# Nine instead of seven of 22 up-projection chunks by seven products, taken in pairs, with weights prepared in two stages

## The chip, the cores and the metric

The kernel runs on one core of a Trainium2 chip. The metric is the device time of one execution in microseconds (us). The core has five engines that each work through a list of their own in order: PE multiplies matrices, DVE does elementwise arithmetic on two operands, ACT does copies and activation functions, POOL and SP here mostly issue DMAs. An engine waits on semaphores for the others. PE writes its results into PSUM, which has eight banks of 128 x 512 f32; everything else is in SBUF.

## The reference, cut to what matters

The program is a decoder trunk of two layers on a residual stream of 512 x 1024. Each layer ends in a gated feed-forward block whose first half is what the change touches:

```python
def conv_ffn(xn, w_up, cw, cb, w_down):
    a = xn @ w_up                      # 512 x 1024 by 1024 x 5632
    T = a.shape[1]
    ap = jnp.pad(a, ((0, 0), (CONV_W - 1, 0), (0, 0)))
    a = sum(ap[:, j:j + T] * cw[j] for j in range(CONV_W)) + cb
    gate, val = jnp.split(a, 2, axis=-1)
    return (jax.nn.gelu(gate, approximate=True) * val) @ w_down
```

All inputs are f32, and the product must keep nearly f32 accuracy.

## The kernel before, in words

**Products.** An f32 operand is split into a high part, rounded to fp32r, and a low part, which is the rest. A product is then three matmuls (`mm3`, L262): high by high, high by low, low by high. Only the third one reads the low part of the weight.

**Chunks.** In `ffn` (L584) the 5632 columns of the up-projection are taken as 22 chunks (`NF`). Chunk c has 128 gate columns and the 128 value columns that belong to them, and a PSUM bank of 128 x 512 for each. A **plain** chunk takes 2 halves x 8 blocks of 128 rows x 3 matmuls = 48 matmuls of 512 columns. Chunks 0 and 1 are made by `first_products`; the loop at L883 makes chunks 2 to 21.

**Seven products.** For the chunks in `SEVEN` (L27: 6, 8, ..., 18) a chunk is a 2 x 2 block product in Strassen's form (Winograd's variant): seven products A11, A12, S1, S2, S3, S4 and A22 of half the rows and half the tokens, each 4 x 3 matmuls of 256 columns (`half_mm`, L863), 84 in all. Their weights are sums and differences of the four blocks of the chunk's weights. `seven_weights` (L650) makes them: raw weights r0 and r1, sums sa and sb (four DVE additions of 512 columns), then four tiles w[0] to w[3] of high parts (ACT copies) and low parts (DVE subtractions). The four output quarters o1 to o4 lie in two banks, and five small DVE additions (L908, L909, L916, L921, L923) with one ACT copy (L906, s1) join the seven products; a product that accumulates onto a quarter can start only when the addition that reads the quarter has run.

**Order within a chunk.** Each engine's order is the program's order (a schedule written by hand). During chunk c the engines also treat the results of chunk c-1: `taps` (L589: per bank one ACT activation, L593, and two DVE multiply-adds, L594 and L596), `glu` (L613, the gelu on ACT) and, a chunk later, `product` (L604, the gate times the value on DVE; the one before goes to DRAM with a POOL DMA, hD, L609). And they prepare the weights of chunk c+2: `weights(c + 2)` is a generator, and each `next(steps)` puts one more step of it into the lists. Near the end of a seven-product chunk PE does the first four blocks of the next plain chunk's first half (`begun`, L917) before S4.

**Weights of plain chunks.** `Weights` (L32) loads raw weights by SP DMAs (L46), 512 KB each, a few ahead; `high` copies the high part on ACT (L54), `low` subtracts on DVE (L62). `high_added` (L81) does without DVE: after the high part ACT writes the negated raw weight, rounded to fp32r, into the place of the low part (L56), and a POOL DMA adds the raw weight to it there (L77, `accum_op=ALU.add`), which leaves the low part. Before the change only chunks 20 and 21 take their weights so, and four weights in the second layer's attention.

**Buffers.** Weight tiles are 8 KB a partition, from a pool of 16 (`t8`); eight of these hold the inputs and their sums during the loop. Raw weights, sa, sb and the taps' bb come from a pool of 10 (`t4`), one of which a gain row holds. A load or a DVE addition that needs a buffer waits until the last reader of an older one is done.

Of the kernel before, what the change touches and what calls it, by code (L numbers as in the profile page):

```python
# [1 line left out]

# [13 lines left out]
T = 512  # L16
# [7 lines left out]
BIG = 3.0e38  # L24


SEVEN = range(6, 19, 2)  # L27
ND = NF // 2
LAST = 3

# [66 lines left out]
def trunk_kernel(ctx, tc, x, norm_gains, w_qkv_a, w_o_a, w_q_b, w_o_b, kv_norm, w_kvf, b_f,  # L97
# [11 lines left out]
    def t8(shape, dt=F32, name="t8"):  # L109
        return p8.tile(shape, dt, tag="t8", name=name)  # L110
# [4 lines left out]
    def t2(shape, dt=F32, name="t2"):  # L115
        return p2.tile(shape, dt, tag="t2", name=name)

    def bank(shape, name="bank"):
        return psp.tile(shape, F32, tag="ps", name=name)
# [464 lines left out]
    def ffn(l, bd, cp, nxt, ahead):  # L584
# [4 lines left out]
        def taps(c, banks, between=None):  # L589
            bb = t4([128, 2, T], name="bb")  # L590
            for s, ch in ((0, c), (1, NF + c)):
                ps = banks[s]
                act.activation(bb[:, s, :], ps, AF.Identity, bias=cp[:, 3, ch:ch + 1], scale=cp[:, 2, ch:ch + 1])  # L593
                dve.scalar_tensor_tensor(bb[:, s, 1:], ps[:, :T - 1], cp[:, 1, ch:ch + 1], bb[:, s, 1:],  # L594
                                         ALU.mult, ALU.add)
                dve.scalar_tensor_tensor(bb[:, s, 2:], ps[:, :T - 2], cp[:, 0, ch:ch + 1], bb[:, s, 2:],  # L596
                                         ALU.mult, ALU.add)
                if s == 0 and between is not None:
                    between()
            return bb  # L600
# [3 lines left out]
        def product():  # L604

            if gated:
                c, bb = gated.pop()
                if c - 1 in hc:
                    pool.dma_start(hD[c - 1], hc.pop(c - 1))  # L609
                hc[c] = t2([128, T], name="hc")  # L610
                dve.tensor_tensor(hc[c], bb[:, 0, :], bb[:, 1, :], ALU.mult)  # L611
# [5 lines left out]
        def post(c, banks, between=None):  # L617
            product()
            glu(c, taps(c, banks, between))
# [4 lines left out]
        def sums_in():  # L624

            v = [t8([128, 4, T], name=f"xsum{i}") for i in range(2)]
            for i in range(2):
                pool.tensor_tensor(v[i], xT[0][i].bitcast(F32), xT[1][i].bitcast(F32), ALU.add)
            yield
            dve.tensor_tensor(v[0][:, :, LO], v[0][:, :, HI], v[0][:, :, LO], ALU.subtract)  # L630
            dve.tensor_tensor(v[0][:, :, HI], v[1][:, :, HI], v[0][:, :, HI], ALU.subtract)
            yield
            dve.tensor_tensor(v[1][:, :, HI], v[1][:, :, HI], v[0][:, :, LO], ALU.subtract)
            dve.tensor_tensor(v[1][:, :, LO], v[1][:, :, LO], v[1][:, :, HI], ALU.subtract)
            yield
            for X, src in ((XA, v[0]), (XB, v[1])):
                X += [t8([128, 4, T], F32R, name="xsh"), t8([128, 4, T], F32R, name="xsl")]
                for k in (0, 2):
                    act.copy(X[0][:, k:k + 2], src[:, k:k + 2])
                    dve.tensor_tensor(X[1][:, k:k + 2], src[:, k:k + 2], X[0][:, k:k + 2].bitcast(F32), ALU.subtract)  # L640
                    yield

        halves = {}

        def split_pair(pair, src, n=1024):
            act.copy(pair[:, 0, :n], src)
            yield
            dve.tensor_tensor(pair[:, 1, :n], src, pair[:, 0, :n].bitcast(F32), ALU.subtract)

        def seven_weights(c):  # L650

            r0, r1 = W.take(2)
            w = [t8([128, 2, 1024], F32R, name="w") for _ in range(4)]
            sa, sb = (t4([128, 1024], name="wsum") for _ in range(2))
            a11, a12, a21, a22 = r0[:, 0:512], r0[:, 512:1024], r1[:, 0:512], r1[:, 512:1024]
            act.copy(w[0][:, 0], r0)
            dve.tensor_tensor(sa[:, 0:512], a11, a21, ALU.subtract)
            dve.tensor_tensor(sb[:, 0:512], a21, a22, ALU.add)
            yield
            dve.tensor_tensor(sa[:, 512:1024], sb[:, 0:512], a11, ALU.subtract)  # L660
            act.copy(w[1][:, 0], sa)
            dve.tensor_tensor(sb[:, 512:1024], a12, sa[:, 512:1024], ALU.subtract)
            yield
            dve.tensor_tensor(w[1][:, 1], sa, w[1][:, 0].bitcast(F32), ALU.subtract)
            act.copy(w[2][:, 0], sb)
            yield
            dve.tensor_tensor(w[0][:, 1], r0, w[0][:, 0].bitcast(F32), ALU.subtract)
            act.copy(w[3][:, 0, 0:512], a22)
            yield
            dve.tensor_tensor(w[2][:, 1], sb, w[2][:, 0].bitcast(F32), ALU.subtract)  # L670
            yield
            dve.tensor_tensor(w[3][:, 1, 0:512], a22, w[3][:, 0, 0:512].bitcast(F32), ALU.subtract)
            v = [t.rearrange("p s (q k c) -> p s q k c", q=2, k=4) for t in w]
            halves[c] = dict(A11=v[0][:, :, 0], A12=v[0][:, :, 1], S3=v[1][:, :, 0], S2=v[1][:, :, 1],
                             S1=v[2][:, :, 0], S4=v[2][:, :, 1], A22=v[3][:, :, 0])

        def plain_weights(c):
            for _ in range(2):
                if c < NF - 2:
                    W.high()  # L680
                    W.low()
                else:
                    W.high_added()
                yield

        def weights(c):
            return seven_weights(c) if c in SEVEN else plain_weights(c)

# [187 lines left out]
        W.ahead = 1  # L878
        W.split(base + 8)
        extra = sums_in()  # L880
        begun = None
        before = None
        for c in range(2, NF):  # L883
            if c == NF - 4:
                pair_load(0)
            if c == NF - 3:
                sums = down_sums([(l, ND - 1), (1, 8 + l)], in_one, pool, 1, 0)
                next(sums)
            steps = weights(c + 2) if c + 2 < NF else iter(())
            banks = [bank([128, T], name="up") for _ in range(2)]  # L890
            if c in SEVEN:
                w = halves.pop(c)
                W.n_get += 2
                x11, x21, x22 = [(xT[0][i], xT[1][i], s) for i, s in ((0, LO), (1, LO), (1, HI))]
                o1, o2, o3, o4 = banks[0][:, LO], banks[0][:, HI], banks[1][:, LO], banks[1][:, HI]
                s1, s12, s17 = (t2([128, 256], name="csum") for _ in range(3))

                def prod(o, a, x, start=False):
                    half_mm(o, w[a], x[0:2], x[2], start)

                prod(o1, "A11", x11, True)
                prod(o2, "S2", (*XB, HI))
                prod(o3, "S3", (*XA, HI), True)
                product()
                bb = taps(*before)
                act.copy(s1, o1)  # L906
                next(steps)
                dve.tensor_tensor(s12, o2, s1, ALU.add)  # L908
                dve.tensor_tensor(s17, o3, s1, ALU.add)  # L909
                glu(before[0], bb)  # L910
                prod(o1, "A12", x21)
                prod(o2, "S1", (*XA, LO))
                prod(o3, "A22", (*XB, LO))
                next(steps)
                next(steps, None)
                dve.tensor_tensor(o4, o2, s17, ALU.add)  # L916
                begun = W.get(), bank([128, T], name="up")  # L917
                up(*begun, range(4))
                prod(o2, "S4", x22)
                next(steps, None)  # L920
                dve.tensor_tensor(o3, o3, s12, ALU.add)  # L921
                next(steps, None)
                dve.tensor_tensor(o2, o2, s1, ALU.add)  # L923
            else:
                for s in range(2):
                    if s == 0 and begun:
                        w, banks[0] = begun
                        up(*begun, range(4, KD))
                        begun = None
                    else:  # L930
                        up(W.get(), banks[s], range(KD))
                    if c == NF - 2:
                        next(sums)
                    if s == 0 and before:
                        post(*before, (lambda: pair_lows(0)) if c == NF - 1 else None)
                        if c >= NF - 2:
                            pair_highs(c - NF + 2)
                            pair_sums(c - NF + 3)
                    next(steps, None)
                    next(extra, None)  # L940
            run(steps)
            before = c, banks
            if c == NF - 3:
                pair_sums(0)
# [725 lines left out]
```

## Time and profile before

| what | value |
|---|---|
| median of three runs | 1122.29 us (1121.77 to 1123.04) |
| the profiled execution's own time | 1126.29 us |
| its span in the profile | 1124.5 us |
| granted PE clock | 0.997 of full speed |
| PE busy | 1110.3 us |
| DVE busy | 892.2 us |
| ACT busy | 614.6 us |
| POOL busy | 183.2 us |

The span runs from the first to the last instruction. Matmuls overlap one another, so the time that one takes from start to end is longer than the distance between two starts; the distance is what counts. In an instruction row the numbers are start and duration in us; in a group row, after the count, busy us and the mean ns of one, then the idle time of the engine ahead of it. In the first layer the loop over chunks 2 to 21 runs from 205.53 to 417.86 us of the span.

### The profile page before, as it was taken

How to read it: one execution, taken by the hardware profiler on the slowest of the kernel's cores; microseconds unless marked ns; L12 is line 12 of the kernel's file. 1: busy time of each engine (PE TensorE's matmuls, PEld its weight loads, DVE VectorE, ACT ScalarE, POOL GpSimd, SP SyncE). 2: the span in 40 equal slices, each digit the busy share in tenths (PEclk: the TensorE clock that was granted, in tenths of full speed). 3: DMA queues.
4: the chain of work that ended last, by engine and by line, in shares of the span. 5: the costliest groups of instructions: out<-in, count | busy, mean ns of one | idle time of the engine just before them, and what ended most of it. 6: DMA issues, size and time to landing. Idle time of an engine off the chain costs nothing.

```text
span 1124.5 us, 17257 instructions
## 1 busy us (share of the span) xinstructions
PE 1110.3 (99%) x6259; PEld 951.7 (85%) x6259; DVE 892.2 (79%) x1453; ACT 614.6 (55%) x1036; POOL 183.2 (16%) x277
## 2 busy tenths in 40 slices
PE   9999999999999999999999999999999999999997
PEld 6988889889899888888788878789989989887886
DVE  6667788888888689997696877748888888689994
ACT  5444575544444556576562678746445445456572
POOL 1832101200000121000001645500300000121000
PEclk9999999999999999999999999999999999999999
DMA  9469854343443699793438666374333433599862
GB/s 322 150 216 409 315 170 134 94 123 113 138 124 114 168 346 377 278 337 104 141 126 305 180 168 156 95 207 122 105 98 118 131 123 121 149 351 371 313 244 75
DMA packets 179183, 217.34 MB, mean 193 GB/s; under 512 B 11225, under 2 KB 131017, under 8 KB 179098
## 3 DMA queue, kind: packets, MB, share of 16 engines
q1 hardware_dynamic: 169594, 183.99, 50.4%
q0 software_dynamic: 9504, 32.25, 8.8%
q8 instruction: 49, 0.80, 0.3%
q14 instruction: 36, 0.29, 0.1%
HBM read 166.08 MB, written 39.63 MB: 183 GB/s over the span
## 4 chain that ended last, share of the span: by engine, by line
PE 83%; DMA 5%; issue 4%; DVE 4%; POOL 2%; ACT 1%; DVEq 0%; POOLq 0%; SPq 0%; ACTq 0%
PE up L263 12%; PE up L264 12%; PE up L265 12%; PE acc L263 8%; PE acc L265 8%; PE acc L264 8%; DMA dact<-hD 3%; PE qk_ps L264 2%; PE qk_ps L263 2%; PE qk_ps L265 2%; PE v_ps L263 2%; PE v_ps L265 2%; PE v_ps L264 2%; POOL bias L1488 1%; PE first L265 1%
## 5 line engine op out<-in xcount | busy, mean ns | idle before, releaser
L593 ACT ACTIVATE bb<-up,conv 128x512 f32<-128x512 f32 x80 | 60.6, 775 | 148.5 <-DVE up L923 76.2
L62 DVE TENSOR_TENSOR w<-wraw,w 128x1024 fp32r<-128x1024 f32 x98 | 125.1, 1305 | 18.3 <-ACT w L54 13.9
L265 PE MATMUL acc<-w 128*128 128x512 f32 (+1 forms) x311 | 120.6, 388 | 0.7 <-DVE w L721 0.7
L263 PE MATMUL acc<-w 128*128 128x512 f32 (+1 forms) x311 | 120.8, 388 | 0.3 <-DVE mix L310 0.3
L54 ACT CAST w<-wraw 128x1024 fp32r<-128x1024 f32 x110 | 111.6, 1047 | 15.6 <-PE v_ps L264 6.9
L263 PE MATMUL up<-xbh,w 128*128 128x512 f32 (+1 forms) x292 | 105.0, 359 | 0.0
L264 PE MATMUL up<-xcl,w 128*128 128x512 f32 (+1 forms) x292 | 104.9, 359 | 0.0
L263 PE MATMUL up<-xch,w 128*128 128x512 f32 (+1 forms) x292 | 104.9, 359 | 0.0
L264 PE MATMUL up<-xbl,w 128*128 128x512 f32 (+1 forms) x292 | 104.9, 359 | 0.0
L265 PE MATMUL up<-xbh,w 128*128 128x512 f32 (+1 forms) x292 | 104.8, 359 | 0.0
L265 PE MATMUL up<-xch,w 128*128 128x512 f32 (+1 forms) x292 | 104.8, 359 | 0.0
L264 PE MATMUL acc<-w 128*128 128x512 f32 (+1 forms) x267 | 103.4, 387 | 0.0
L609 POOL DMA_DIRECT2D hD<-hc x42 | 24.2, 577 | 316.8 <-DVE hc L611 316.6
L265 PEld LDWEIGHTS acc<-w 128*128 128x128 f32 x311 | 58.4, 188 | 13.0 <-DVE w L721 1.1
L263 PEld LDWEIGHTS acc<-w 128*128 128x128 f32 x311 | 58.4, 188 | 12.5 <-DVE mix L310 0.7
L594 DVE SCALAR_TENSOR_TENSOR bb<-up,conv,bb 128x511 f32<-128x511 f32 x80 | 59.5, 744 | 7.7 <-ACT bb L593 7.7
L265 PE MATMUL up<-xsh,w 128*128 128x256 f32 x224 | 63.5, 283 | 0.0
L264 PE MATMUL up<-xsl,w 128*128 128x256 f32 x224 | 63.5, 283 | 0.0
L263 PE MATMUL up<-xsh,w 128*128 128x256 f32 x224 | 63.5, 283 | 0.0
L263 PEld LDWEIGHTS up<-xbh,w 128*128 128x128 f32 x292 | 55.1, 189 | 8.3
L596 DVE SCALAR_TENSOR_TENSOR bb<-up,conv,bb 128x510 f32<-128x510 f32 x80 | 59.9, 749 | 2.8
L265 PEld LDWEIGHTS up<-xch,w 128*128 128x128 f32 x292 | 55.1, 189 | 8.3
(303 smaller groups left out, 3023.3 us busy)
## 6 DMA issues: line engine op xcount, KB each, us to landing
wraw<-in_w_up_dram SPq DMA_DIRECT2D x88, 512.0 KB
dT<-dsums SPq DMA_DIRECT2D x24, 512.0 KB
dsums<-in_w_down_dram SPq DMA_DIRECT2D x22, 512.0 KB
dsums<-in_w_down_dram SPq DMA_DIRECT2D x44, 256.0 KB
hD<-hc POOLq DMA_DIRECT2D x44, 256.0 KB, 4.7
dact<-hD SPq DMA_DIRECT2D x44, 256.0 KB
wraw<-dT SPq DMA_DIRECT2D x22, 512.0 KB
wraw<-in_w_down_dram SPq DMA_DIRECT2D x22, 512.0 KB
```

What stands on the lines that cost most here:

```text
L54: self.nc.scalar.copy(pair[:, 0], raw)
L62: self.nc.vector.tensor_tensor(pair[:, 1], raw, pair[:, 0].bitcast(F32), ALU.subtract)
L263: pe.matmul(o, ah, bh, start=first, stop=False, skip_group_check=shared)
L264: pe.matmul(o, ah, bl, start=False, stop=False, skip_group_check=shared)
L265: pe.matmul(o, al, bh, start=False, stop=last, skip_group_check=shared)
L593: act.activation(bb[:, s, :], ps, AF.Identity, bias=cp[:, 3, ch:ch + 1], scale=cp[:, 2, ch:ch + 1])
L594: dve.scalar_tensor_tensor(bb[:, s, 1:], ps[:, :T - 1], cp[:, 1, ch:ch + 1], bb[:, s, 1:], ALU.mult, ALU.add)
L596: dve.scalar_tensor_tensor(bb[:, s, 2:], ps[:, :T - 2], cp[:, 0, ch:ch + 1], bb[:, s, 2:], ALU.mult, ALU.add)
L609: pool.dma_start(hD[c - 1], hc.pop(c - 1))
L1488: pool.tensor_scalar(bias[:, hh, :n], cks[j][:, hh, :n], -1.0, cq[:, i, hd:hd + 1], ALU.mult, ALU.add)
```

## The change

`SEVEN` becomes 6, 8, 9, 11, 12, 14, 15, 17, 18: nine chunks per layer, of which eight stand in pairs with one plain chunk between pairs. Four more chunks in the two layers together are made by seven products.

In a pair the second chunk is begun within the first: its A11 and S3 stand between S1 and S4 of the first, where a chunk followed by a plain one has the four blocks of `begun`. The order of the seven is now A11, S3, S2, A22, A12, S1, S4, and S3, S2 and s17 of a chunk that isn't begun are issued within `taps`, ahead of the second bank's taps.

The weights come in two stages: `weights_a(c + 2)` makes w[0] and w[1], `weights_b(c + 1)` makes w[2] and w[3] a chunk later. The low parts of the first chunk of a pair (and of chunk 6) are made by `add_low`, which is ACT (negated) and an adding POOL DMA, except A22's; in the second chunk of a pair only sb's (S1 and S4) are. A plain chunk's first half is made by `high_added`, its second by `high` and `low`; both halves by `high_added` in chunks 4, 5, 20 and 21. In the first chunk of a pair the steps for the plain chunk after the pair that are still left at its end go into the second chunk's list.

The diff, cut to its core:

```diff
-SEVEN = range(6, 19, 2)
+SEVEN = 6, 8, 9, 11, 12, 14, 15, 17, 18
...
+        def add_low(w, raw):
+            act.activation(w[:, 1], raw, AF.Copy, scale=-1.0)
+            pool.dma_start(w[:, 1], raw, accum_op=ALU.add)
+
+        def sub_low(w, raw, n=1024):
+            dve.tensor_tensor(w[:, 1, :n], raw, w[:, 0, :n].bitcast(F32), ALU.subtract)
+
+        def weights_a(c):
+            if c >= NF:
+                return
+            if c not in SEVEN:
+                for i in range(2):
+                    if i == 0 or c < SEVEN[0] or c >= NF - 2:
+                        W.high_added()
+                    else:
+                        W.high()
+                        W.low()
+                    yield
+                return
             r0, r1 = W.take(2)
...
             act.copy(w[0][:, 0], r0)
+            if c - 1 not in SEVEN:
+                add_low(w[0], r0)
             dve.tensor_tensor(sa[:, 0:512], a11, a21, ALU.subtract)
             dve.tensor_tensor(sb[:, 0:512], a21, a22, ALU.add)
             yield
             dve.tensor_tensor(sa[:, 512:1024], sb[:, 0:512], a11, ALU.subtract)
+            if c - 1 not in SEVEN:
+                act.copy(w[1][:, 0], sa)
+                add_low(w[1], sa)
...
+        def weights_b(c):
+            if c not in SEVEN:
+                return
+            (w0, w1), r0, a12, a22, sa, sb = rest.pop(c)
+            if c - 1 in SEVEN:
+                act.copy(w1[:, 0], sa)
+                sub_low(w0, r0)
+            w = [t8([128, 2, 1024], F32R, name="w") for _ in range(2)]
             dve.tensor_tensor(sb[:, 512:1024], a12, sa[:, 512:1024], ALU.subtract)
+            act.copy(w[1][:, 0, 0:512], a22)
+            if c - 1 in SEVEN:
+                sub_low(w1, sa)
             yield
+            act.copy(w[0][:, 0], sb)
+            add_low(w[0], sb)
+            sub_low(w[1], a22, 512)
...
-            steps = weights(c + 2) if c + 2 < NF else iter(())
+            steps = chain(steps, weights_b(c + 1), weights_a(c + 2))
             if c in SEVEN:
...
+                def begin():
+                    act.copy(s1, o1)
+                    prod(o3, "S3", (*XA, HI), True)
+                    dve.tensor_tensor(s17, o3, s1, ALU.add)
+                    prod(o2, "S2", (*XB, HI))
+
+                def join():
+                    dve.tensor_tensor(s12, o2, s1, ALU.add)
+
+                if begun:
+                    prod(o2, "S2", (*XB, HI))
+                    product()
+                    join()
+                    bb = taps(*before)
+                else:
+                    prod(o1, "A11", x11, True)
+                    product()
+                    bb = taps(*before, begin)
+                    join()
+                prod(o3, "A22", (*XB, LO))
                 prod(o1, "A12", x21)
                 prod(o2, "S1", (*XA, LO))
-                prod(o3, "A22", (*XB, LO))
-                next(steps)
+                next(steps, None)
+                glu(before[0], bb)
                 next(steps, None)
                 dve.tensor_tensor(o4, o2, s17, ALU.add)
-                begun = W.get(), bank([128, T], name="up")
-                up(*begun, range(4))
+                if c + 1 in SEVEN:
...
+                    prod(b1, "A11", x11, True, halves[c + 1])
+                    act.copy(begun[1], b1)
+                    prod(b3, "S3", (*XA, HI), True, halves[c + 1])
+                else:
+                    begun = W.get(), bank([128, T], name="up")
+                    up(*begun, range(4))
                 prod(o2, "S4", x22)
                 next(steps, None)
                 dve.tensor_tensor(o3, o3, s12, ALU.add)
-                next(steps, None)
+                if c + 1 in SEVEN:
+                    dve.tensor_tensor(begun[2], b3, begun[1], ALU.add)
+                else:
+                    next(steps, None)
                 dve.tensor_tensor(o2, o2, s1, ALU.add)
...
-            run(steps)
+            if c + 1 not in SEVEN or c + 2 in SEVEN:
+                run(steps)
```

More of the change, by code (lines that the diff above doesn't have):

```diff
@@ L1 @@
 from contextlib import ExitStack
+from itertools import chain
 import concourse.bass as bass
@@ L641, in sums_in @@
                     yield
-        halves = {}
+        halves, rest = {}, {}
         def split_pair(pair, src, n=1024):
@@ L648, in split_pair @@
             dve.tensor_tensor(pair[:, 1, :n], src, pair[:, 0, :n].bitcast(F32), ALU.subtract)
-        def seven_weights(c):
+        def add_low(w, raw):
[15 more added lines that the diff above has]
+                return
             r0, r1 = W.take(2)
-            w = [t8([128, 2, 1024], F32R, name="w") for _ in range(4)]
+            w = [t8([128, 2, 1024], F32R, name="w") for _ in range(2)]
             sa, sb = (t4([128, 1024], name="wsum") for _ in range(2))
@@ L660, in seven_weights @@
             dve.tensor_tensor(sa[:, 512:1024], sb[:, 0:512], a11, ALU.subtract)
-            act.copy(w[1][:, 0], sa)
+            if c - 1 not in SEVEN:
+                act.copy(w[1][:, 0], sa)
+                add_low(w[1], sa)
+            v = [t.rearrange("p s (q k c) -> p s q k c", q=2, k=4) for t in w]
+            halves[c] = dict(A11=v[0][:, :, 0], A12=v[0][:, :, 1], S3=v[1][:, :, 0], S2=v[1][:, :, 1])
+            rest[c] = w, r0, a12, a22, sa, sb
+        def weights_b(c):
[5 more added lines that the diff above has]
+                sub_low(w0, r0)
+            w = [t8([128, 2, 1024], F32R, name="w") for _ in range(2)]
@@ L662, in seven_weights @@
             dve.tensor_tensor(sb[:, 512:1024], a12, sa[:, 512:1024], ALU.subtract)
+            act.copy(w[1][:, 0, 0:512], a22)
+            if c - 1 in SEVEN:
+                sub_low(w1, sa)
             yield
-            dve.tensor_tensor(w[1][:, 1], sa, w[1][:, 0].bitcast(F32), ALU.subtract)
-            act.copy(w[2][:, 0], sb)
-            yield
-            dve.tensor_tensor(w[0][:, 1], r0, w[0][:, 0].bitcast(F32), ALU.subtract)
-            act.copy(w[3][:, 0, 0:512], a22)
-            yield
@@ L670, in seven_weights @@
[L670 to L684, printed above, removed]
@@ L686, in weights @@
-        def weights(c):
-            return seven_weights(c) if c in SEVEN else plain_weights(c)
+            act.copy(w[0][:, 0], sb)
+            add_low(w[0], sb)
+            sub_low(w[1], a22, 512)
+            v = [t.rearrange("p s (q k c) -> p s q k c", q=2, k=4) for t in w]
+            halves[c].update(S1=v[0][:, :, 0], S4=v[0][:, :, 1], A22=v[1][:, :, 0])
+            yield
         acts, one, two, raws, later2 = {}, {}, {}, {}, {}
@@ L880, in ffn @@
         extra = sums_in()
+        steps = iter(())
         begun = None
@@ L888, in ffn @@
                 next(sums)
-            steps = weights(c + 2) if c + 2 < NF else iter(())
-            banks = [bank([128, T], name="up") for _ in range(2)]
+            steps = chain(steps, weights_b(c + 1), weights_a(c + 2))
             if c in SEVEN:
@@ L894, in ffn @@
                 x11, x21, x22 = [(xT[0][i], xT[1][i], s) for i, s in ((0, LO), (1, LO), (1, HI))]
+                if begun:
+                    banks, s1, s17 = begun
+                else:
+                    banks = [bank([128, T], name="up") for _ in range(2)]
+                    s1, s17 = (t2([128, 256], name="csum") for _ in range(2))
+                s12 = t2([128, 256], name="csum")
                 o1, o2, o3, o4 = banks[0][:, LO], banks[0][:, HI], banks[1][:, LO], banks[1][:, HI]
-                s1, s12, s17 = (t2([128, 256], name="csum") for _ in range(3))
@@ L898, in prod @@
-                def prod(o, a, x, start=False):
+                def prod(o, a, x, start=False, w=w):
                     half_mm(o, w[a], x[0:2], x[2], start)
[L901 to L906, printed above, removed]
-                next(steps)
-                dve.tensor_tensor(s12, o2, s1, ALU.add)
-                dve.tensor_tensor(s17, o3, s1, ALU.add)
@@ L910, in ffn @@
-                glu(before[0], bb)
+                def begin():
[5 more added lines that the diff above has]
+                    dve.tensor_tensor(s12, o2, s1, ALU.add)
+                if begun:
+                    prod(o2, "S2", (*XB, HI))
[7 more added lines that the diff above has]
+                    join()
@@ L911, in ffn @@
+                prod(o3, "A22", (*XB, LO))
                 prod(o1, "A12", x21)
                 prod(o2, "S1", (*XA, LO))
-                prod(o3, "A22", (*XB, LO))
-                next(steps)
+                next(steps, None)
+                glu(before[0], bb)
                 next(steps, None)
                 dve.tensor_tensor(o4, o2, s17, ALU.add)
-                begun = W.get(), bank([128, T], name="up")
-                up(*begun, range(4))
+                if c + 1 in SEVEN:
+                    begun = ([bank([128, T], name="up") for _ in range(2)],
+                             *(t2([128, 256], name="csum") for _ in range(2)))
+                    b1, b3 = (o[:, LO] for o in begun[0])
+                    prod(b1, "A11", x11, True, halves[c + 1])
[4 more added lines that the diff above has]
+                    up(*begun, range(4))
@@ L921, in ffn @@
                 dve.tensor_tensor(o3, o3, s12, ALU.add)
-                next(steps, None)
+                if c + 1 in SEVEN:
+                    dve.tensor_tensor(begun[2], b3, begun[1], ALU.add)
+                else:
+                    next(steps, None)
                 dve.tensor_tensor(o2, o2, s1, ALU.add)
             else:
+                banks = [bank([128, T], name="up") for _ in range(1 if begun else 2)]
+                if begun:
+                    w, first = begun
+                    banks = [first, *banks]
                 for s in range(2):
                     if s == 0 and begun:
-                        w, banks[0] = begun
                         up(*begun, range(4, KD))
@@ L934, in ffn @@
                     if s == 0 and before:
-                        post(*before, (lambda: pair_lows(0)) if c == NF - 1 else None)
+                        product()
+                        bb = taps(*before, (lambda: pair_lows(0)) if c == NF - 1 else None)
+                        next(steps, None)
+                        glu(before[0], bb)
                         if c >= NF - 2:
```

## The prediction

> **What bounds the kernel now.** First the page: its head, the clock and the chain that ended last.
>
> ```profile
> span 1124.5 us, 17257 instructions
> ...
> PE 1110.3 (99%) x6259; PEld 951.7 (85%) x6259; DVE 892.2 (79%) x1453; ACT 614.6 (55%) x1036; POOL 183.2 (16%) x277
> ...
> PEclk9999999999999999999999999999999999999999
> ...
> PE 83%; DMA 5%; issue 4%; DVE 4%; POOL 2%; ACT 1%; DVEq 0%; POOLq 0%; SPq 0%; ACTq 0%
> PE up L263 12%; PE up L264 12%; PE up L265 12%; PE acc L263 8%; PE acc L265 8%; PE acc L264 8%; DMA dact<-hD 3%; PE qk_ps L264 2%; PE qk_ps L263 2%; PE qk_ps L265 2%; PE v_ps L263 2%; PE v_ps L265 2%; PE v_ps L264 2%; POOL bias L1488 1%; PE first L265 1%
> ```
>
> PE is busy 99% of the span at full clock, and the largest part of the chain, 36%, is the up-projection's three matmul lines. Next the windows: four plain chunks, one seven-product chunk with a plain one behind it, and six of the seven products alone. The first number is the stretch, then PE's busy time, PEld, DVE, ACT, POOL.
>
> ```profile
> 205.53:249.08 43.55, 43.55 (x195) 36.07 (x193) 37.56 (x43) 22.11 (x27) 2.18 (x4) 1.00 0.34 105
> 270.08:291.09 21.01, 21.01 (x134) 19.09 (x132) 17.72 (x26) 9.79 (x13) 1.08 (x2) 1.00 0.42 126
> 249.08:257.71 8.63, 8.63 (x73) 8.63 (x72) 6.29 (x10) 5.15 (x7) 0.00 (x0) 1.00 0.32 93
> ```
>
> PE's busy time equals each stretch: it never waits there. The waits say the same from the other side: in this loop DVE and ACT wait for PE's products.
>
> ```profile
> ACT bb L593 <- DVE up L923: 76.2, 14, 5.7
> ACT bb L593 <- PE up L265: 72.3, 30, 4.7
> ...
> DVE up L923 <- PE up L265: 20.4, 14, 3.3
> ```
>
> So a saving in PE's work counts in full, and so does any new wait of PE.
>
> **What the seven products save.** A plain chunk takes 43.55 / 4 = 10.89 us. The pair of chunks takes 21.01, so a seven-product chunk takes 10.12 by difference. By its parts one product is 8.63 / 6 = 1.44 us, and seven are 10.07. The saving is 0.77 to 0.82 us a chunk; four more chunks save **3.1 to 3.3 us, I take 3.2**. That is all that this change can give: 0.29%.
>
> **DVE, ACT and DMA in a cycle.** A cycle of the new loop (two seven-product chunks, one plain) is 2 x 10.07 + 10.94 (the rest of 21.01) = 31.1 us of PE. DVE's prices are from the groups of one old period:
>
> ```profile
> L594 DVE SCALAR_TENSOR_TENSOR bb<-up,conv,bb 128x511 f32<-128x511 f32 x5 | 3.7, 744 | 0.0
> L596 DVE SCALAR_TENSOR_TENSOR bb<-up,conv,bb 128x510 f32<-128x510 f32 x4 | 3.0, 748 | 0.1
> L611 DVE TENSOR_TENSOR hc<-bb 128x512 f32<-128x512 f32 x2 | 1.4, 688 | 0.0
> L667 DVE TENSOR_TENSOR w<-wraw,w 128x1024 fp32r<-128x1024 f32 x1 | 1.2, 1218 | 0.0
> L657 DVE TENSOR_TENSOR wsum<-wraw 128x512 f32<-128x512 f32 x1 | 0.7, 683 | 0.0
> L909 DVE TENSOR_TENSOR csum<-up,csum 128x256 f32<-128x256 f32 x1 | 0.4, 425 | 0.3 <-PE up L265 0.3
> ```
>
> Taps and product are 3 x (2 x 0.744 + 2 x 0.748 + 0.688) = 11.0; joins 10 x 0.425 = 4.3; sums and A22's lows 10 x 0.683 = 6.8; lows of 1024 columns, two in the second chunk and one in the plain one, 3 x 1.218 = 3.7. That is 25.8 us of 31.1, or 83%, where the old period has 17.72 of 21.01, or 84%. DVE stays free enough only because five lows per cycle go to ACT and an adding DMA. For ACT that is five more activations:
>
> ```profile
> 294.16 0.37 ACT L906 COPY csum<-up 128x256 f32<-128x256 f32 x1 [2.09 <-PE up L265]
> 294.43 1.05 ACT L656 CAST w<-wraw 128x1024 fp32r<-128x1024 f32 x1
> ```
>
> ```profile
> 378.43 1.05 ACT L54 CAST w<-wraw 128x1024 fp32r<-128x1024 f32 x1
> 379.38 1.06 ACT L56 ACTIVATE w<-wraw 128x1024 fp32r<-128x1024 f32 x1
> ...
> 381.80 1.06 ACT L56 ACTIVATE w<-wraw 128x1024 fp32r<-128x1024 f32 x1
> ```
>
> Old ACT time is 9.79 per 21.01, so 14.7 per 31.5; five more at 1.06 and one more chunk's copies make about 22 of 31.1. The software queue took 8.8% of 16 engines' span for 32.25 MB, which is 3.1 us per MB:
>
> ```profile
> q0 software_dynamic: 9504, 32.25, 8.8%
> ```
>
> Five adds of 0.52 MB are then 8 us a cycle, 26% on top of the 0.42 of the window above. No engine and no queue is full. What is left is whether each low part lands in time.
>
> **The adding DMAs.** The rows are POOL's issues, then the time from issue to landing (min, median, max) over all twelve adds, then the same over the four in the attention of layer two, which go one at a time, where PE waited for one:
>
> ```profile
> 383.15 0.86 POOL L77 DMA_DIRECT2D w<-wraw  x1 [1.25 <-ACT w L56]
> ```
>
> ```profile
> DMA to landing us min/median/max: 6.2/8.4/10.2
> ```
>
> ```profile
>   PE q_ps L265: 2.1, 2
> busy tenths in 40 slices 0000000000000000000000000000000000000000
> DMA to landing us min/median/max: 6.2/7.4/8.7
> ```
>
> An add is issued 0.3 us after ACT's negated copy (381.80 + 1.06 to 383.15). I put PE's list of a pair on one time line, with A11 of the first chunk at 0 and 1.44 a product: S3 1.44, S2 2.88, A22 4.31, A12 5.75, S1 7.19, then the second chunk's A11 8.63 and S3 10.07, S4 11.51; second chunk S2 12.94, A22 14.38, A12 15.82, S1 17.26; first four blocks of the plain chunk 18.70, S4 21.45.
>
> *The plain chunk's first half.* Its `high_added` stands in ACT's list behind the copy s1 of the second chunk, and that copy waits for A11 to end at 10.07. PE's end to ACT's start is 0.2 us, as here, where PE's products of the next chunk start at 291.09:
>
> ```profile
> 291.29 0.78 ACT L593 ACTIVATE bb<-up,conv 128x512 f32<-128x512 f32 x1 [1.82 <-PE up L265]
> ```
>
> So s1 starts at 10.27, the high copy 0.27 later (294.16 to 294.43) at 10.54, the negated copy 0.95 later (378.43 to 379.38) at 11.49, ending 12.55; the add is issued at 12.85. PE reads the low part with its third matmul at 18.70 + 2 x 0.23 = 19.15 (0.23 is 10.89 / 48). The add has **6.3 us**. Its rows give 6.2, 7.4 or 8.4, and 10.2: a wait of nothing, 1.1, 2.1 or 3.9 us. It is nearest to the adds that go one at a time, since the add before it (sb's, at 9.4) is 3.4 us ahead: I take 7.4, a wait of **1.1 us in each pair**. Behind it PE has the rest of the plain chunk and all that follows; nothing there gives it back. POOL's next entry, a write of hD, comes later, and nobody waits for it soon.
>
> *The sums' adds.* sb of the second chunk: DVE's last sum before it ends near 7.0 (S3 ends 2.88, then s17, two taps, s12, one low, one sum at the prices above); two ACT copies and 0.3 make the issue 9.4. S1's third matmul is at 17.5: 8.1 us. In the first chunk the chain runs from S4 of the chunk before through four taps to an issue about 0.7 us ahead of A11; S1 needs it at 7.4: 8.1 us again. Against 7.4 both are hidden; at 8.4 each costs 0.3, at 10.2 2.1. I take nothing and keep these. r0 and sa of the first chunk have more than 9 us.
>
> *Moved reads.* A22 now comes right after S2 and overwrites the quarter that s17 reads: s17 ends about 3.5, A22 starts 4.31. A12 needs s12 read: 5.3 to 5.4 against 5.75. Covered by 0.8 and 0.35 us; if DVE is later than that, each pair pays the excess.
>
> *Buffers.* Between a first chunk's sums and the next there are thirteen requests per cycle for nine free `t4` buffers. Loads wait for releases already:
>
> ```profile
> SPq L46 <- DVE w L664: 117.0, 14, 11.4
> ```
>
> By the same order three loads of raw weights follow the second chunk's lows at 7 to 9 us, so they lie ahead of sb's add. That is why I don't take the 6.2.
>
> **The sum.** Eight pairs: 8 x 1.1 = 8.8 us of new waits, less 3.2 saved, is +5.6 us. The profiled execution took 1126.3 (its span and 1.8 around it), 4.0 above the median of the runs, 1122.3. I put the change on the median: **1127.9, say 1128 us**.
>
> **The rivals.** *The adds land in time* (34%): all within 6.3 us. For it: one of twelve did (6.2), and DMA is 0.42 busy. Then only the saving is left: 1122.3 - 3.2 = **1119**, faster. It decides at a wait of 0.4 us a pair, where the saving is used up. By the Trainium skill, page "DMA: Bandwidth & Descriptors", section "Anatomy of one DMA — SWDGE (gpsimd) path", a DMA from POOL takes 2.0 us plus its bytes at 436 GB/s, which for 0.52 MB is an estimate of 3.2 us; by that rule nothing waits and 1119 comes out. Not one of this trace's adds is near it: the fastest took 6.2.
>
> *The adds queue* (12%): behind the three loads and behind each other, as in the pairs of adds for chunks 20 and 21, up to 10.2. Then the plain half waits 3.9 a pair and S1 up to 2.1: 8 x 3.9 - 3.2 = +28, **1150**, more with S1.
>
> *A draw* (12%): waits of 0.15 to 0.65 us a pair, **1122**.
>
> *DVE late for A12* (part of the forecast's upper half): 1 us more on DVE between S3 and s12 would cost 0.65 a pair, +5.2 in all, **1133** with the forecast's waits. Against it: DVE waits for S3 at that place, so its backlog is gone.
>
> **How the numbers follow.** The forecast, waits of 0.65 to 2.2 us a pair (1124.5 to 1137), has 42%; in time 34%, a draw 12%, queueing 12%. From the fastest case, 1119 with half a us for the runs' own spread (1121.8 to 1123.0), to 1141, where the plain half waits 2.1 (the 8.4) and both S1 adds 0.3: 8 x 2.7 - 3.2 = +18.4. The range is 1118.5 to 1141; above it lies most of the queueing. Within 0.2% (2.2 us, about what a measurement of this kernel can tell) are waits of 0.13 to 0.68 us a pair: 13%; faster 35%; slower 52%.
>
> **What would show it.** Right: PE idle ahead of an up matmul at L265, ended by a DMA that writes w from wraw, eight times, about 1 us each; L77's landings 7 to 8 us; seven-product chunks 10.1 us and the span's other parts as before. S1's wait would stand at a DMA that writes w from wsum. In time: PE busy equal to every stretch of the loop and cycles of 31.1 us. Wrong: waits of PE on DVE (s12, s17) or on ACT (s1), landings under 6.3 or over 10 us, or a wait of DVE or SP for buffers that moves the sums.

## The result, and the profile after

The changed kernel takes 1137.96 us (median of four runs, 1136.81 to 1139.06) against 1122.66 (1121.77 to 1123.22): slower, with a ratio on record of 1.0114 and a 95% interval of 1.0093 to 1.0134. The two medians alone give 1.0136, and a later comparison gave 1.0130 (1.0112 to 1.0147). Between the medians are 15.3 us, between the profiled executions 12.8 (spans 1137.3 and 1124.5): the one of the kernel before took 3.6 us more than its median, that of the changed kernel 1.1 more. The sign was forecast and the time lies in the range, but a loss of 5.6 us was predicted, and two thirds of the 15.3 were missed.

The head of the page, the clock, and the software queue:

```profile
span 1137.3 us, 17794 instructions
...
PE 1111.5 (98%) x6403; PEld 955.4 (84%) x6403; DVE 854.5 (75%) x1441; ACT 675.1 (59%) x1104; POOL 229.6 (20%) x333
...
PEclk9999999999999999999999999999999999999999
...
q0 software_dynamic: 17568, 61.61, 23.3%
...
PE 29%; DMA 7%; issue 2%; POOL 2%; DVE 1%; ACT 1%; DVEq 0%; POOLq 0%; SPq 0%; ACTq 0%
```

The clock is as before. The chain's shares can't be compared with those of before: followed back from the end, the chain of this trace breaks off at 648.63 us of the span, so its shares add up to 42% only, and the first layer's loop isn't in it. So here is the loop itself, from chunk 6 to its end in both layers, first in the kernel before, then in the changed one:

```profile
249.08:417.86 168.78, 168.78 (x1022) 151.64 (x1021) 135.50 (x197) 80.62 (x105) 15.34 (x26) 1.00 0.53 164
842.66:1011.43 168.77, 168.77 (x1022) 151.63 (x1021) 134.52 (x196) 80.80 (x105) 15.32 (x26) 1.00 0.53 165
```

```profile
249.10:425.22 176.12, 169.56 (x1093) 153.57 (x1092) 126.77 (x201) 105.76 (x134) 34.71 (x49) 1.00 0.90 230
850.03:1024.21 174.18, 169.11 (x1094) 153.53 (x1092) 126.06 (x200) 105.59 (x134) 34.37 (x49) 1.00 0.91 230
```

The two loops together take 12.75 us more, which is all of the spans' difference, and PE is idle in them for 11.6 us. What PE waits for, in the waits of PE (total us, times, longest):

```profile
PE up L266 <- DMA w<-wraw: 6.1, 9, 1.1
PE up L266 <- DMA w<-wsum: 5.5, 7, 1.2
```

The matmul lines moved down by one: L266 is the third matmul of `mm3`, which reads the low part. Nine waits are for low parts of plain chunks' first halves, seven for sums. Before, the loop had none: PE's busy time was equal to the stretch. Three cycles (pair and plain chunk), and the last pair's 13 products, in which PE waits for nothing:

```profile
271.21:304.26 33.05, 31.63 (x217) 29.13 (x216) 23.92 (x39) 20.46 (x27) 5.99 (x10) 1.00 0.85 200
304.26:337.08 32.82, 31.63 (x217) 29.14 (x216) 23.93 (x39) 20.45 (x27) 5.98 (x10) 1.00 0.87 201
337.08:370.44 33.36, 31.63 (x217) 29.13 (x216) 24.02 (x39) 20.45 (x27) 5.97 (x10) 1.00 0.84 197
970.03:988.74 18.71, 18.71 (x158) 18.71 (x156) 13.50 (x21) 12.38 (x17) 2.90 (x5) 1.00 0.97 229
```

A product still takes 18.71 / 13 = 1.44 us, so the saving is there. A cycle takes 33.1 instead of 31.1. Here are both waits of the first of these cycles, in PE's order of time:

```profile
288.48 0.28 PE L264 MATMUL up<-xsh,w 128*128 128x256 f32 x1
288.60 0.28 PE L265 MATMUL up<-xsl,w 128*128 128x256 f32 x1
289.71 0.38 PE L266 MATMUL up<-xsh,w 128*128 128x256 f32 x1 [0.83 <-DMA w<-wsum]
289.93 0.28 PE L264 MATMUL up<-xsh,w 128*128 128x256 f32 x1
...
291.23 0.40 PE L265 MATMUL up<-xbl,w 128*128 128x512 f32 x1
292.22 0.50 PE L266 MATMUL up<-xbh,w 128*128 128x512 f32 x1 [0.59 <-DMA w<-wraw]
292.55 0.40 PE L264 MATMUL up<-xbh,w 128*128 128x512 f32 x1
```

The first stands 17.4 us after the pair's start at 271.21: S1 of the second chunk. The second is the plain chunk's first half. The rows also show that a wait costs more than its idle time: from 288.60 to 289.71 are 1.11 us where 0.12 is usual, 0.99 more for 0.83 idle, because a running matmul covers the start of the wait, and the next step (289.71 to 289.93) is 0.10 longer as well. So 11.6 us of idle in 16 waits are about 11.6 + 16 x 0.26 = 15.8 us of time; less the 3.2 saved that is 12.6, the spans' 12.8.

SP's loads, then POOL's issues of these two adds, then how long each add was under way until it landed:

```profile
278.33 2.09 SPq L47 DMA_DIRECT2D wraw<-in_w_up_dram  x3
```

```profile
280.61 0.85 POOL L654 DMA_DIRECT2D w<-wsum  x1 [8.77 <-DVE up L954]
284.05 0.86 POOL L78 DMA_DIRECT2D w<-wraw  x1 [2.59 <-ACT w L57]
```

```profile
L654 POOL DMA_DIRECT2D w<-wsum x1: 854/854/854, 280.6 to 280.6; - x1
...
DMA to landing us min/median/max: 9.1/9.1/9.1
```

```profile
L78 POOL DMA_DIRECT2D w<-wraw x1: 865/865/865, 284.0 to 284.0; - x1
...
DMA to landing us min/median/max: 8.1/8.1/8.1
```

The issues are at 9.40 and 12.84 us of the cycle, where the prediction put them (9.4 and 12.85). What it got wrong is how long the first add is under way: 9.1 us, with three loads issued in the 2.3 us ahead of it. What the DMA engines do after its issue shows why. From 280.61 to 284.50 all packets are of SP's queue, q1, and not one is of the software queue, which carries the adds:

```profile
q1 hardware_dynamic: 1734, 0.87, 81.1%
```

The first chunk's second sums' add, sb's, has no such loads ahead:

```profile
L654 POOL DMA_DIRECT2D w<-wsum x1: 854/854/854, 303.5 to 303.5; - x1
...
DMA to landing us min/median/max: 5.6/5.6/5.6
```

### The profile page after: what moved, and what is told of

It is laid out like the page before. It is cut to its first block, busy times and chain, and to the rows that moved or that the text cites. A ratio compares the mean times of both kernels' runs of the same rounds, so it can differ in the third digit from the quotient of the medians.

```text
span 1137.3 us, 17794 instructions
## 1 busy us (share of the span) xinstructions
PE 1111.5 (98%) x6403; PEld 955.4 (84%) x6403; DVE 854.5 (75%) x1441; ACT 675.1 (59%) x1104; POOL 229.6 (20%) x333
## 3 DMA queue, kind: packets, MB, share of 16 engines
q0 software_dynamic: 17568, 61.61, 23.3%
## 5 line engine op out<-in xcount | busy, mean ns | idle before, releaser
L266 PE MATMUL acc<-w 128*128 128x512 f32 (+1 forms) x311 | 120.7, 388 | 1.8 <-DVE w L744 1.8
L55 ACT CAST w<-wraw 128x1024 fp32r<-128x1024 f32 x102 | 104.9, 1048 | 15.7 <-PE v_ps L265 6.9
L266 PE MATMUL up<-xbh,w 128*128 128x512 f32 (+1 forms) x284 | 99.7, 351 | 3.7 <-DMA w<-wraw 3.7
L266 PE MATMUL up<-xch,w 128*128 128x512 f32 (+1 forms) x284 | 99.7, 351 | 2.4 <-DMA w<-wraw 2.4
L265 PE MATMUL up<-xbl,w 128*128 128x512 f32 (+1 forms) x284 | 99.3, 350 | 0.0
L265 PE MATMUL up<-xcl,w 128*128 128x512 f32 (+1 forms) x284 | 99.2, 349 | 0.0
L264 PE MATMUL up<-xch,w 128*128 128x512 f32 (+1 forms) x284 | 99.2, 349 | 0.0
L264 PE MATMUL up<-xbh,w 128*128 128x512 f32 (+1 forms) x284 | 99.2, 349 | 0.0
L63 DVE TENSOR_TENSOR w<-wraw,w 128x1024 fp32r<-128x1024 f32 x72 | 87.3, 1236 | 14.7 <-ACT w L55 14.2
L266 PE MATMUL up<-xsh,w 128*128 128x256 f32 x288 | 82.2, 286 | 5.5 <-DMA w<-wsum 5.5
L264 PE MATMUL up<-xsh,w 128*128 128x256 f32 x288 | 81.5, 283 | 0.0
L265 PE MATMUL up<-xsl,w 128*128 128x256 f32 x288 | 81.5, 283 | 0.0
L78 POOL DMA_DIRECT2D w<-wraw x30 | 28.0, 938 | 221.1 <-ACT w L57 207.9
L266 PEld LDWEIGHTS acc<-w 128*128 128x128 f32 x311 | 58.4, 188 | 14.4 <-DVE w L744 2.6
L266 PEld LDWEIGHTS up<-xbh,w 128*128 128x128 f32 x284 | 53.7, 189 | 12.7 <-DMA w<-wraw 5.9
L266 PEld LDWEIGHTS up<-xch,w 128*128 128x128 f32 x284 | 53.7, 189 | 11.1 <-DMA w<-wraw 4.4
```

Of the source, the lines that this page charges most:

```text
L55: self.nc.scalar.copy(pair[:, 0], raw)
L63: self.nc.vector.tensor_tensor(pair[:, 1], raw, pair[:, 0].bitcast(F32), ALU.subtract)
L78: self.nc.gpsimd.dma_start(pair[:, 1], raw, accum_op=ALU.add)
L264: pe.matmul(o, ah, bh, start=first, stop=False, skip_group_check=shared)
L265: pe.matmul(o, ah, bl, start=False, stop=False, skip_group_check=shared)
L266: pe.matmul(o, al, bh, start=False, stop=last, skip_group_check=shared)
```

## The experiments

The theory: the loss is all in adds that land late, and they are late because of what lies ahead of them, three loads of raw weights ahead of sb's add and sb's add ahead of the plain half's. The rivals: an add takes 8 to 9 us by itself; DVE is the limit wherever the low parts are made; the loads aren't what holds the add. In the comparisons of the first three experiments the kernel before took 1125.33 us (22 runs, 1122.61 to 1127.77). The ratios are against that; the expected times start from the first comparison, where the kernel before took 1122.7.

**The plain half's low part on DVE.**

```diff
-                    if i == 0 or c < SEVEN[0] or c >= NF - 2:
+                    if c < SEVEN[0] or c >= NF - 2:
                         W.high_added()
```

> Edit: the plain chunk after a pair has both low parts made on DVE (high and low), none by an adding DMA; the sums' adds stay. Theory (late adds): the waits at the plain chunk's first half, nine of 0.5 to 1.3 us and 8.5 us in all in the changed kernel's profile, go; those at S1 of the second chunk, 7.4 us in all, stay. 1138.0 - 8.5 = 1129.5 us, 1127 to 1131. Rival (DVE is the limit, and the low part is late wherever it is made): PE waits for a DVE low part instead, 1135 or more.

Measured: 1129.24 us (seven runs, 1126.83 to 1132.70), ratio 1.0034 (1.0019 to 1.0049). The plain halves' waits are gone, and of S1's seven six are left:

```profile
PE up L266 <- DMA w<-wsum: 5.0, 6, 1.1
```

So S1's wait doesn't hang on the plain half's add, and DVE isn't the limit here. The add of sb, with no other add behind it, still took 8.7 us at the same place of the cycle:

```profile
L654 POOL DMA_DIRECT2D w<-wsum x1: 852/852/852, 279.6 to 279.6; - x1
...
DMA to landing us min/median/max: 8.7/8.7/8.7
```

**sb's low part of the second chunk on DVE.**

```diff
             act.copy(w[0][:, 0], sb)
-            add_low(w[0], sb)
+            if c - 1 in SEVEN:
+                sub_low(w[0], sb)
+            else:
+                add_low(w[0], sb)
```

> Edit: in the second chunk of a pair sb's low part is made on DVE, so that only the add of the plain chunk's first half is left between the pair's A11 and the plain chunk. Theory (the adds queue behind one another and behind the loads): S1's waits go and the plain half's add, with none ahead of it, lands about 2 to 3 us sooner; its wait is 0 to 0.5 us a pair. 1120 to 1126 us. Rival (an add takes 8 to 9 us whatever is in the queue): the wait that S1 no longer has comes back at the plain half, because its need moves ahead by as much; 2 us a pair stay, 1134 to 1139.

Measured: 1127.17 us (ten runs, 1125.41 to 1130.20), ratio 1.0022 (1.0010 to 1.0034), a little over the 1120 to 1126 of the theory. In its profile S1's waits and the plain halves' are gone together. The plain half's add is issued at the same place of the cycle but now has none ahead of it; two of them:

```profile
L78 POOL DMA_DIRECT2D w<-wraw x2: 842/847/852, 314.3 to 345.4; - x2
...
DMA to landing us min/median/max: 5.3/5.3/5.3
```

5.3 us instead of 8.1: an add hasn't a time of its own of 8 to 9 us, and the rival falls. DMA is busy as before in this cycle, 0.83, and PE waits for nothing:

```profile
270.10:301.18 31.08, 31.08 (x218) 29.16 (x217) 25.04 (x40) 19.50 (x26) 5.12 (x8) 1.00 0.83 195
```

Over both loops the DMA engines' share is 0.90, as in the changed kernel. So it isn't the total load that costs, but what is ahead of the one add. Why this kernel is slower than the next by half a per cent is only partly seen. It isn't the loop, which from chunk 6 on takes 334.45 us in both layers together, against 334.16 in the next. Its profile has waits for DVE of 4.0 us at the start of the down-projection, where the next has 0.9, and its span is 3.2 us longer; the medians differ by 5.0, and the rest stays open.

**Both.** The two edits together.

> Both edits together: no add is left that PE needs soon; DVE makes 2.4 us more per cycle of 31.1. Theory (late adds are all of the loss): no wait of PE in the loop, cycles of 31.1 us, 1122.7 - 3.2 = 1119.5, 1118.5 to 1122. Rival (DVE becomes the limit; it has 25.8 + 2.4 = 28.2 of 31.1 by the rows): PE waits for s12, s17 or low parts, over 1125.

Measured: 1122.14 us (eight runs, 1120.03 to 1124.44) beside 1125.33 for the kernel before on that chip: ratio 0.9972 (0.9961 to 0.9983), **faster than both kernels**. Against the kernel before that is 3.2 us (1.9 to 4.4 by the interval), which is the saving that the products were predicted to give. The time is just above the expected 1118.5 to 1122; from 1125.33 the same sum gives 1122.1. A cycle of it, and the loop from chunk 6 on in both layers:

```profile
270.10:301.20 31.10, 31.10 (x218) 29.18 (x217) 26.05 (x40) 18.55 (x25) 4.32 (x8) 1.00 0.74 178
```

```profile
249.09:416.17 167.08, 167.08 (x1094) 153.77 (x1092) 135.89 (x209) 97.24 (x125) 26.53 (x39) 1.00 0.82 213
841.45:1008.53 167.08, 167.08 (x1093) 153.75 (x1092) 137.26 (x211) 96.96 (x125) 26.60 (x39) 1.00 0.82 213
```

A cycle takes 31.1 us, PE is never idle, and DVE is busy for 26.05. The two loops take 3.4 us less than in the kernel before. It keeps the other adds, those of the first chunk's three low parts, which have time.

**The changed kernel without the loads.** Chunks 9 to 19 take chunk 8's raw weights again.

```diff
-            add_cols(w_up[l], c * 128)
-            add_cols(w_up[l], DFF + c * 128)
+            for first in (c * 128, DFF + c * 128):
+                if 8 < c < 20:
+                    again[len(pieces)] = len(pieces) - 2 * (c - 8)
+                    add(lambda raw: [])
+                else:
+                    add_cols(w_up[l], first)
...
+        if n in again:
+            return kept[again[n]]
```

> The changed kernel, but chunks 9 to 19 of each layer take chunk 8's raw weights, which stay in their buffers, so that no weights are loaded for these chunks (this part of the computation is changed). All adds stay. Theory (the loads that lie ahead hold the adds up): sb's add of the second chunk takes 5.5 to 6.5 us instead of 8.6 to 9.4, and no wait at S1 or the plain half is over 0.3 us; span 1120 to 1123. Rival (the add is slow by itself, or DVE and ACT hold up its descriptors): it still takes 8 to 9 us, span 1135 to 1138.

Measured: one run, 1123.95 us, span 1122.2, beside 1137.3 for the changed kernel's. The adds of the sums (nine) and of the plain halves (three) in cycles of the first layer whose loads are gone:

```profile
L664 POOL DMA_DIRECT2D w<-wsum x9: 847/854/869, 279.2 to 362.3; - x9
...
DMA to landing us min/median/max: 4.5/4.6/5.7
```

```profile
L78 POOL DMA_DIRECT2D w<-wraw x3: 862/862/867, 282.7 to 344.9; - x3
...
DMA to landing us min/median/max: 4.6/4.6/5.1
```

All adds of the changed kernel are there, at the same places, and PE waits for none of these. They are faster than the expected 5.5 to 6.5 us. The add of sb that took 9.1 us in the changed kernel is issued here at 279.24; its packets begin 1.4 us later, and until it lands at 283.80 they keep the 16 engines busy for 60.8% of 4.56 us, 2.8 us:

```profile
q0 software_dynamic: 144, 0.52, 60.8%
```

What waits are left belong to the last pair of each layer (chunks 17 and 18), where loads for chunks 20 and 21 and for the down-projection still lie ahead; they are longer than the expected 0.3 us:

```profile
PE up L276 <- DMA w<-wraw: 2.3, 2, 1.2
...
PE up L276 <- DMA w<-wsum: 1.1, 2, 0.6
```

Together with the packets of the changed kernel this shows that the loads made the adds late. The kernel also needs fewer buffers than the changed one, but its adds are issued at the same distance from the pair's start, so that isn't what made them land sooner.

**No adds in the pairs.** On top of both edits the first chunk's three low parts are made on DVE:

```diff
-            act.activation(w[:, 1], raw, AF.Copy, scale=-1.0)
-            pool.dma_start(w[:, 1], raw, accum_op=ALU.add)
+            sub_low(w, raw)
```

> Edit: on top of both edits of the third experiment the first chunk's three low parts (r0, sa, sb) are made on DVE too; the only adding DMAs left are those of plain chunks 4, 5, 20 and 21. Theory (DVE has room for two more low parts, not for five): DVE's work in a cycle is 25.8 + 5 x 1.22 = 31.9 us against 31.1 of PE, so PE waits for DVE; at least 0.8 us a cycle in eight cycles and more where the additions of a pair are late: 1126 to 1136. Rival (the adds were never needed; the prices of DVE overlap by about 0.08 us an instruction, so that it fits): no more waits than in the third experiment, 1119 to 1122.

Measured: 1134.82 us (four runs), ratio 1.0093 (1.0076 to 1.0110), within the theory's 1126 to 1136, but not by its count: DVE is busy 29.27 us of a cycle, less than the 31.9 worked out, and the cycle is 33.21.

```profile
301.91:335.12 33.21, 31.86 (x218) 29.18 (x216) 29.27 (x44) 15.99 (x22) 1.62 (x3) 1.00 0.40 119
```

DVE isn't full; it is late at certain places, above all at one. PE waits for s17, the addition ahead of A22:

```profile
PE up L264 <- DVE csum L934: 6.8, 6, 1.1
```

Two shorter waits stand in the rows of PE's weight loads (PEld), for o4's addition (L956) and s12's (L938):

```profile
PEld up L264 <- DVE up L956: 3.4, 6, 0.6
...
PEld up L264 <- DVE csum L938: 2.1, 8, 0.3
```

In this cycle the three cost 1.4, 0.4 and 0.3 us by the distances of PE's starts, which is its 2.1 us over 31.1. In DVE's order of time, sb's low part of the first chunk waits 1.12 us for ACT's copy, and the sums, product and taps behind it are late; s17 runs at 307.05, where PE's S3 ended near 301.91 + 2.88 = 304.8:

```profile
301.33 1.23 DVE L656 TENSOR_TENSOR w<-wsum,w 128x1024 fp32r<-128x1024 f32 x1 [1.12 <-ACT w L704]
...
305.00 0.68 DVE L612 TENSOR_TENSOR hc<-bb 128x512 f32<-128x512 f32 x1
...
307.05 0.41 DVE L934 TENSOR_TENSOR csum<-up,csum 128x256 f32<-128x256 f32 x1
```

So the adding DMAs are worth having: without any in the pairs the kernel loses 10.4 us to the kernel before in its comparison (1124.45), with those of the first chunk alone it gains 3.2.

**The changed kernel again.**

> The changed kernel again, beside the runs of the kernel before on the same chip, to compare with the edits: PE's waits for adds of 12.5 to 16 us in all in its profile, less 3.2 saved, 1.008 to 1.014 of the kernel before. Rival (the first measurement's 15.3 us holds more than waits for adds): a ratio over 1.013 with waits that sum to less.

Measured: 1138.50 us (four runs), 1.0130 (1.0112 to 1.0147); waits in its profile 8.0 us for w<-wraw (9 times) and 6.7 for w<-wsum (7 times), 14.7 of idle, which with 16 x 0.26 is 18.9; less 3.2 is 15.7. Its loops from chunk 6 on (248.94 to 424.88 and 849.29 to 1026.66) take 15.76 us more than those of the kernel before. The waits differ from run to run by some us, and they carry the loss.

## Why the prediction missed the size

- **The saving** (3.2 us, four chunks at 0.77 to 0.82): right. The version without late adds has it, 3.2 us on the chip and 3.4 in the two loops of its trace.
- **DVE, ACT and DMA in a cycle**: right that none is full. DVE was put at 25.8 of 31.1 and is busy 23.9 of 33.05. The adds' load was sized wrong: 3.1 us per MB gave 1.6 us of the 16 engines for one. The queue's share went from 8.8% of 1124.5 to 23.3% of 1137.3, 166 us for 56 more adds, 3.0 each, and one alone took 2.8. A cycle's DMA share is 0.85, not 0.68. By itself that cost nothing, as the second experiment shows.
- **The plain half's wait**: right in place and, by luck, in size. Eight were predicted at 1.1; nine came (chunk 7, behind the lone chunk 6 in the first layer, was overlooked), 6.1 us of idle, 8.4 of time with 0.26 each, against 8.8. But two errors cancel: the add took 8.1 (not 7.4), and its need had moved back by 1.1 us with the wait at S1. The cause was only in part the predicted one: the prediction took the 7.4 of an add that goes alone, and this one was late because sb's add was ahead of it. Without that it took 5.3, and there was no wait.
- **The sums' adds**: here the prediction failed. "Against 7.4 both are hidden", it says, and "I take nothing": the first chunk's is hidden (5.6 us), the second chunk's isn't: 9.1 against 8.1 to spare, and in the two layers seven waits, 5.5 us of idle, 7.3 of time. The term was put at zero and measured 7.3 us, three quarters of the 10 us that the prediction missed. Another 2.5 are no wait: the medians differ by 15.3, the profiled executions, in which the waits were read, by 12.8.
- **Why it failed**: one latency was taken from rows of other places (the adds that go one at a time, 7.4) and put on every add. But the same text had the order of the buffers and three loads "ahead of sb's add", and used them only against the 6.2. Rows of adds with loads beside them (8.2 to 9.8 for chunks 20 and 21 in the first layer) fitted sb's better, and a later queue entry should have been set behind the one ahead of it. What an add takes follows from what is ahead: 4.6 with nothing, 5.3 with loads that are nearly through, 8.6 to 9.4 behind three loads in seven of the changed kernel's eight pairs (7.2 in the last).
- **The rival "the adds queue"** (12%, 1150): its mechanism is what the runs show, sb's add behind three loads and the plain half's behind sb's. Its sizes were too large: it put 3.9 us a pair at the plain half alone, and the waits of a pair, S1's included, cost 1.8 on average (10.8 us of idle and 15 x 0.26, in eight pairs).
- **The rival "the adds land in time"**, 1119 against 1122.3: its gain of 3.2 us is what came out once no add was late, 1122.14 against 1125.33. The rule of the Trainium skill, page "DMA: Bandwidth & Descriptors", section "Anatomy of one DMA — SWDGE (gpsimd) path", 2.0 us and the bytes at 436 GB/s, an estimate of 3.2 us for 0.52 MB, doesn't hold for these adds, of which the fastest, with nothing ahead, takes 4.5.
- **"DVE late for A12"**: no wait of PE on DVE in the changed kernel's loop. It came when all adds were taken out of the pairs, above all at A22, and with 0.3 us a cycle at A12.

## What to carry to other kernels

Before a DMA is put between a producer and an engine that never waits, list what every queue will hold at its issue, and take its latency from a row with the same things ahead of it; a median over unlike places says little. Move work to such a DMA where there is slack (here three low parts of the first chunk, with 8 us and more and a quiet queue), and leave on the compute engine the piece with the least. Here sixteen waits of about 1 us each cost five times what the arithmetic saved.

## What the runs showed of the hardware

An adding DMA of 0.52 MB within SBUF keeps the 16 DMA engines busy for 2.8 us alone (60.8% of 4.56 us) and 3.0 on average (166 us for 56), and lands 4.5 to 5.7 us after its issue in the cycles without loads. With three loads of 0.52 MB issued by SP in the 2.3 us before, it lands after 8.6 to 9.4 us in most pairs (7.2 in the changed kernel's last, 6.9 and 7.6 in two of the first experiment). In the cycle shown none of its packets moves in the 3.9 us after its issue, while SP's queue moves 0.87 MB: the loads, though they stand in another queue, went first. A short wait of PE for an add costs about 0.26 us more than the idle time that the profile shows for it, in the rows above 0.99 + 0.10 us of time for 0.83 of idle.
